# Weaving score steps with the transposes and values of other blocks, and leaving one softmax map undivided, in a two-layer attention and MLP trunk

## The chip, the cores and the metric

The kernel runs on one core of one Trainium2 chip. A core has a matrix engine (PE; its weight loads are listed apart as PEld), a vector engine (DVE), an activation engine (ACT), a general engine (POOL) and a queue for transfers (SP). Each takes its instructions in the order of its own queue; semaphores hold an instruction back until what it needs is there. Matrix products land in eight banks of a small memory (PSUM), each 128 x 512 numbers of 32 bits, and have to be read out by DVE or ACT before a bank is used again. The metric is the time of one execution in microseconds, the median of several.

## The reference

The input x has 512 tokens of 1024 numbers in float32. Each of two layers normalizes x, projects it, runs two kinds of attention heads on the parts, projects their joined outputs and adds them to x, and then adds a squared-ReLU MLP of width 4096. One more normalization follows at the end.

```python
h = rmsnorm(x, attn_norm[l])
sb_q, sb_k, sb_v, df_q, df_k, df_v = split(h @ w_in[l])       # 512 wide each
# stick-breaking heads (8 of 64): z = q k / 8, strictly causal
w = exp(log_sigmoid(z) + (sum over later keys of log_sigmoid(-z)))
sb_out = w @ v
# differential heads (4 of 2 x 64, values of 128), q and k rotated, causal by chunks of 64
p = softmax(s)                                                # two maps, p[0] and p[1]
attn = p[0] - lam * p[1]
df_out = rmsnorm(attn @ v, subln_norm[l]) * (1 - lambda_init)
x = x + concat(sb_out, df_out) @ w_o[l]
x = x + square(relu(rmsnorm(x, mlp_norm[l]) @ w_ff1[l])) @ w_ff2[l]
```

`rmsnorm(y)` is y / sqrt(mean(y * y) + 1e-6) times a gain.

## The kernel before

All of x stays on the chip, transposed: 8 tiles of 128 features by 512 tokens. To keep float32 accuracy on PE, an operand is split into a rounded high part (ACT, `split`, L207; weights L119) and the rest (DVE, L208; weights L120), and a product is three matmuls (`three`, L257 to L262): high by high, high by low, low by high. A projection block (`block`) takes one weight tile of 128 x 1024 through 8 such triples into a bank with the tag "mm". Weight tiles are loaded by SP three ahead and split two ahead.

A layer starts with the attention stage. A generator `dense` gives the projection blocks in the order of `ORDER`: for the four differential blocks b = 0 to 3 queries with keys (d) and values (w), then for the four stick-breaking blocks queries, keys (s) and values (u), and after them half of the output projection (`wo(1)`). When a projection is done, it is taken out of its bank. For d this is a rotation: DVE makes two products (L463, L464), POOL a difference and a sum (L472, then L471), ACT and DVE split the results, SP moves query and low key parts into stacked tiles (L437), and ACT copies the high key parts (L458). Values are transposed on PE (vT, L405), and split by ACT and DVE (L412, L413).

A second generator, `attn`, runs over 24 units: 8 differential ones (block b, half of the queries) and 16 stick-breaking ones (block, head, half). A unit goes through three parts. `s1` makes the scores for two query rows of 128 (S, L499 and L500; bank tag "s", two banks) and turns them into weights. For a differential unit (`s1_df`) DVE masks the scores (L539, L543) and takes the negated row maximum (L540, L544); ACT takes Exp and sums the row (L552); DVE takes the reciprocals of both sums (L558) and multiplies the second with minus lambda (L559); POOL multiplies map 0 with its reciprocal (L560); DVE adds the scaled map 1 (L561). For a stick-breaking unit ACT takes two sigmoids (L514, L515), DVE a running product (L517), POOL the final product (L520). `s2` transposes the weights on PE (T, L580; bank tag "t", two banks) and splits them; a unit of the first half has three transposes, one of the second half seven in two steps of four and three. `s3` multiplies them with the values (O, L608 to L611; tag "o"). In iteration i, `attn` runs `s1` of unit i, `s2` of unit i - 2 and `s3` of unit i - 3. After a differential block's two halves are through, its output is normalized over two iterations: `start_norm` calls `rms_a` (squares transposed on PE, rs_d; sums and scaling on DVE, L232 and L233; the power -1/2 on POOL, L238; its split on DVE, chi and clo, L239 and L240; two diagonals on POOL, L243 and L245), and `finish` spreads the result with two matmuls (rb_d, L253 and L254), a copy on ACT, a product on POOL (L660) and a split.

The loop at L739 weaves the two generators: after each dense triple `attn` gets a credit, and steps of `attn` are taken while it is positive. A `yield 0` means that what it needs isn't there yet. The text's order is not yet that of the queues: the framework's scheduler orders each engine's instructions by its own estimates of their times.

After the attention stage come the other half of the output projection (`wo(0)`) and the MLP (f, at 128 x 512 per matmul throughout).

Of the kernel before, what the change touches and what calls it, by code (L numbers as in the profile page):

```python
# [9 lines left out]
F32 = mybir.dt.float32  # L10
# [3 lines left out]
ALU = mybir.AluOpType  # L14
# [127 lines left out]
def trunk(ctx, tc, xT, w, gains, lamv, cos, sin, out):  # L142
# [83 lines left out]

    def rms_a(src, inv_n, col, name, eng, dgt):
        pt = bank("t", "rs_" + name)
        if RST and eng is not nc.gpsimd or RST == 2:
            for j in range(4):  # L230
                nc.tensor.transpose(pt[:, j * P : (j + 1) * P], src[:, j * P : (j + 1) * P], ident)
            nc.vector.tensor_reduce(out=ms, in_=pt.rearrange("p (j f) -> p j f", j=4), axis=AX.X, op=ALU.add)  # L232
            nc.vector.tensor_scalar(out=ms, in0=ms, scalar1=inv_n, scalar2=EPS, op0=ALU.mult, op1=ALU.add)  # L233
        else:
# [116 lines left out]
    for l in range(L):  # L351
        with ExitStack() as actx:
# [66 lines left out]
            dgs = {}  # L419
            heads = {}  # L420

            later = []
# [101 lines left out]
            def s1_df(u):  # L524
                b, half = u["b"], u["half"]
                st = {w: stacks[("d", b, w)] for w in "qk"}
                u["w"] = []
                for i in (2 * half, 2 * half + 1):
                    wd = P * (i + 1)
                    nm = f"{l}d{b}{i}"  # L530
                    sm = a3.tile([P, 6], F32, tag="sm", name="sm" + nm, bufs=4)
                    pr = []
                    both = bank("s", f"S{nm}") if wd <= 256 else None
                    for m in range(2):
# [13 lines left out]
                        if both is None or m == 1:  # L548
                            for mm, (pp, ss) in enumerate(pr):
                                if both is None and mm < m:  # L550
                                    continue
                                nc.scalar.activation(  # L552
                                    pp[:, 0:wd], ss[:, 0:wd], AF.Exp, bias=sm[:, mm : mm + 1],
                                    accum_out=sm[:, 2 + mm : 3 + mm])
                        if m == 0 and both is None:
                            yield max(wd, 256) * 2 * MMC
                    pr = [pp for pp, _ in pr]
                    nc.vector.reciprocal(sm[:, 4:6], sm[:, 2:4])  # L558
                    nc.vector.tensor_mul(sm[:, 5:6], sm[:, 5:6], nlam[:, l : l + 1])  # L559
                    nc.gpsimd.tensor_mul(pr[0][:, 0:wd], pr[0][:, 0:wd], sm[:, 4:5].to_broadcast([P, wd]))  # L560
                    nc.vector.scalar_tensor_tensor(  # L561
                        out=pr[0][:, 0:wd], in0=pr[1][:, 0:wd], scalar=sm[:, 5:6], in1=pr[0][:, 0:wd],
                        op0=ALU.mult, op1=ALU.add)
# [87 lines left out]
            def start_norm():  # L651
                b, os_, sqo, rc = late[0]
                dgs[b] = rms_a(sqo, 1.0 / P, rc, f"d{l}{b}", nc.gpsimd, tr)
                return 0.43

            def finish():
# [5 lines left out]
                return 0.43  # L662

            def attn():
                n = len(units)
                stage = 0
                for i in range(n + LAG3):
                    stage = stage + 1 if late else 0
                    if i < n:
                        u = units[i]  # L670
                        while not ok((u["kind"], u["b"])):
                            yield 0
                        yield from (s1_sb if u["kind"] == "s" else s1_df)(u)
                    if stage == 1:
                        yield start_norm()
                    if 0 <= i - LAG2 < n:
                        yield from s2(units[i - LAG2])
                    if stage == 2:
                        yield finish()
                        stage = 0  # L680
                    if 0 <= i - LAG3 < n:
                        while not ok(("v" + units[i - LAG3]["kind"], units[i - LAG3]["b"])):
                            yield 0
                        yield from s3(units[i - LAG3])

# [195 lines left out]
```

## Time and profile before

| | |
|---|---|
| median of 3 runs | 1228.05 us (1227.83 to 1228.29) |
| the profiled execution's own time | 1228.06 us |
| its span, first to last instruction | 1226.3 us |
| PE busy | 1194.8 us (97%), 5658 matmuls |
| DVE busy | 680.1 us (55%), 1016 instructions |
| ACT busy | 551.6 us (45%), 932 |
| POOL busy | 202.3 us (16%), 260 |

The span by stage, with PE's busy time in each:

| stage | us | PE busy |
|---|---|---|
| opening and first projections | 0 to 37 | 34.2 |
| layer 0, differential scores | 37 to 128.5 | 84.7 |
| layer 0, stick-breaking scores beside projections | 128.5 to 205.6 | 74.5 |
| layer 0, output projection | 205.6 to 262 | 56.4 of 56.4 |
| layer 0, MLP | 262 to 612 | 350 of 350 |
| layer 1, first projections | 612 to 640 | 28 of 28 |
| layer 1, differential scores | 640 to 728.5 | 82.1 |
| layer 1, stick-breaking scores | 728.5 to 805.6 | 74.5 |
| layer 1, output projection and MLP | 805.6 to 1200 | all |
| end | 1200 to 1226.3 | 16.0 |

Names in the profile: S0d is a score bank of layer 0 for differential heads, T1s a bank of transposes of layer 1 for stick-breaking heads, p0w2v a projection block (layer 0, values of block 2). A line such as "L552 p0d<-S0d" is the source line, what is written and what is read. Matmuls are pipelined: one of 128 x 512 is listed with 389 ns, but in a full stream the next starts 227 ns later. The granted clock is 1.00 where PE runs at full speed.

### The profile page before, as it was taken

Reading aid. Unit: us, or ns where it says so; the run is one execution under the profiler, and the core shown is the slowest. Engines: PE = TensorE matmul, PEld = TensorE weight load, DVE = VectorE, ACT = ScalarE, POOL = GpSimd, SP = SyncE. Lnnn points to the kernel's source line nnn. Section 1 sums busy time; section 2 is a strip of 40 time slices with the busy share of each in tenths; the row PEclk is TensorE's granted clock in tenths of the full one; section 3 lists DMA queues with packets and bytes.
Section 4 is the critical chain, followed back from the end, with each engine's and each line's share of the span. In section 5 each row is a group of like instructions: output and inputs, shape, how many; then the busy total and the mean of one; then the engine's idle time right before and its main releaser. Section 6 shows DMA issues by size and latency. Waiting matters only on the chain.

```text
span 1226.3 us, 15312 instructions
## 1 busy us (share of the span) xinstructions
PE 1194.8 (97%) x5658; PEld 991.6 (81%) x5658; DVE 680.1 (55%) x1016; ACT 551.6 (45%) x932; POOL 202.3 (16%) x260
## 2 busy tenths in 40 slices
PE   9989999999999999999998999999999999999996
PEld 6777878888888888888887788888888888888886
DVE  7778877764532334433367887886544322544325
ACT  5666665553431234423347765665443221443114
POOL 1313543230000000001122344432100000000002
PEclk9999999999999999999999999999999999999998
DMA  7344443222233232232234344432223233232221
GB/s 250 78 137 133 119 136 104 68 87 104 87 102 101 88 103 95 94 104 90 100 97 132 110 128 118 123 103 70 94 96 103 89 101 103 86 103 91 90 95 69
DMA packets 46890, 128.16 MB, mean 105 GB/s; under 512 B 7264, under 2 KB 10336, under 8 KB 46816
## 3 DMA queue, kind: packets, MB, share of 16 engines
q1 hardware_dynamic: 46672, 127.17, 33.0%
q8 instruction: 45, 0.74, 0.2%
q14 instruction: 29, 0.24, 0.1%
q10 hardware_dynamic: 144, 0.02, 0.0%
HBM read 104.09 MB, written 2.10 MB: 87 GB/s over the span
## 4 chain that ended last, share of the span: by engine, by line
PE 85%; DVE 4%; ACT 3%; POOL 2%; issue 1%; SPq 1%; DMA 0%; DVEq 0%; POOLq 0%; ACTq 0%
PE f L260 19%; PE f L262 19%; PE f L261 19%; PE wo L261 2%; PE wo L260 2%; PE wo L262 2%; DVE wlo L120 1%; SPq L437 1%; PE T1s L580 1%; PE T0s L580 1%; PE O1s L609 0%; PE O0s L609 0%; PE O1s L608 0%; PE O0s L608 0%; PE S1d L499 0%
## 5 line engine op out<-in xcount | busy, mean ns | idle before, releaser
L119 ACT ACTIVATE whi<-raw 128x1024 fp32r<-128x1024 f32 (+2 forms) x198 | 203.2, 1028 | 480.0 <-PE f L261 427.2
L120 DVE TENSOR_TENSOR wlo<-raw,whi 128x1024 fp32r<-128x1024 f32 (+2 forms) x198 | 242.0, 1224 | 147.1 <-ACT whi L119 146.2
L260 PE MATMUL f<-h_hi,whi 128*128 128x512 f32 x512 | 199.4, 389 | 0.0
L262 PE MATMUL f<-h_hi,wlo 128*128 128x512 f32 x512 | 199.2, 389 | 0.0
L261 PE MATMUL f<-h_lo,whi 128*128 128x512 f32 x512 | 199.2, 389 | 0.0
L260 PE MATMUL f<-uh,whi 128*128 128x512 f32 x496 | 192.9, 389 | 0.0
L261 PE MATMUL f<-ul,whi 128*128 128x512 f32 x496 | 192.9, 389 | 0.0
L262 PE MATMUL f<-uh,wlo 128*128 128x512 f32 x496 | 192.9, 389 | 0.0
L783 DVE SCALAR_TENSOR_TENSOR ft<-f,rbc 128x512 f32<-128x512 f32 x64 | 44.3, 692 | 163.8 <-PE f L262 162.8
L262 PEld LDWEIGHTS f<-h_hi,wlo 128*128 128x128 f32 x512 | 96.1, 188 | 20.1
L261 PEld LDWEIGHTS f<-h_lo,whi 128*128 128x128 f32 x512 | 96.1, 188 | 20.0
L260 PEld LDWEIGHTS f<-h_hi,whi 128*128 128x128 f32 x512 | 96.1, 188 | 19.8
L261 PEld LDWEIGHTS f<-ul,whi 128*128 128x128 f32 x496 | 93.1, 188 | 19.4
L262 PEld LDWEIGHTS f<-uh,wlo 128*128 128x128 f32 x496 | 93.1, 188 | 19.4
L260 PEld LDWEIGHTS f<-uh,whi 128*128 128x128 f32 x496 | 93.1, 188 | 19.2
L221 POOL TENSOR_TENSOR ssq<-ssq,sq 128x512 f32<-128x512 f32 x21 | 34.8, 1656 | 374.3 <-ACT sq L220 365.2
L812 DVE TENSOR_TENSOR x<-x,f 128x512 f32<-128x512 f32 x32 | 22.0, 688 | 103.0 <-PE f L262 103.0
L342 POOL TENSOR_TENSOR ssq<-ssq,sqf 128x256 f32<-128x256 f32 x6 | 4.4, 737 | 338.4 <-ACT sqf L340 335.0
L208 DVE TENSOR_TENSOR ul<-fu,uh 128x512 fp32r<-128x512 f32 x64 | 44.1, 692 | 0.4 <-ACT uh L207 0.4
L207 ACT ACTIVATE uh<-fu 128x512 fp32r<-128x512 f32 x64 | 40.6, 635 | 2.0
L784 ACT ACTIVATE fu<-ft 128x512 f32<-128x512 f32 x64 | 39.7, 620 | 1.6 <-DVE ft L783 1.6
L520 POOL TENSOR_TENSOR sig1s<-sig1s,C1s 128x128 f32<-128x128 f32 (+3 forms) x32 | 30.0, 939 | 55.3 <-DVE C1s L517 40.9
(725 smaller groups left out, 2173.5 us busy)
## 6 DMA issues: line engine op xcount, KB each, us to landing
raw<-in_w SPq DMA_DIRECT2D x176, 512.0 KB, 3.5
raw<-in_w SPq DMA_DIRECT2D x16, 448.0 KB, 3.1
x<-in_xT SPq DMA_DIRECT2D x8, 256.0 KB, 4.4
out_xT<-y SPq DMA_DIRECT2D x8, 256.0 KB, 2.4
raw<-in_w SPq DMA_DIRECT2D x8, 128.0 KB, 4.3
cos_t<-in_cos SPq DMA_DIRECT2D x2, 256.0 KB, 3.8
sin_t<-in_sin SPq DMA_DIRECT2D x2, 256.0 KB, 3.6
kl0d0k<-l0d0k SPq DMA_DIRECT2D x8, 64.0 KB, 2.0
```

The source lines that it names most:

```text
L119: h = nc.scalar.activation(hi[:, a:b], raw[:, a:b], AF.Copy)
L120: self.last = h, nc.vector.tensor_tensor(out=lo[:, a:b], in0=raw[:, a:b], in1=hi[:, a:b].bitcast(F32), op=ALU.subtract)
L207: nc.scalar.activation(hi, src, AF.Copy)
L208: nc.vector.tensor_tensor(out=lo, in0=src, in1=hi.bitcast(F32), op=ALU.subtract)
L221: return s, eng.tensor_tensor(out=ssq, in0=ssq, in1=sq, op=ALU.add)
L260: nc.tensor.matmul(pt, ah, bh, start=first, stop=False)
L261: nc.tensor.matmul(pt, ah, bl, start=False, stop=False)
L262: nc.tensor.matmul(pt, al, bh, start=False, stop=last)
L520: nc.gpsimd.tensor_mul(sig[:, 0:wd], sig[:, 0:wd], C[:, 1 : wd + 1])
L580: nc.tensor.transpose(pt[:, off : off + P], u["w"][qi][:, kb * P : (kb + 1) * P], ident)
L783: nc.vector.scalar_tensor_tensor(out=t, in0=pt, scalar=0.0, in1=rbc, op0=ALU.max, op1=ALU.mult)
L784: nc.scalar.activation(uu, t, AF.Square)
```

## The change

Two things are changed, both in the attention stage.

In `attn`, the parts of an iteration ran one after the other: all of `s1` of unit i, then the start of a norm, then `s2` of unit i - 2, then the end of a norm, then `s3` of unit i - 3. Now everything behind `s1` is a generator of its own, `behind_scores`, and one step of it is taken after each step of `s1`. What is left of it follows after the last one. The number of steps and what they compute are as before.

In `s1_df`, the maps are no longer divided by the first sum. Where the weights were e0 / t0 - lam e1 / t1, with e the exponentials and t their row sums, they are now e0 - lam (t0 / t1) e1, which is t0 times as much. POOL's multiplication of map 0 falls away; DVE takes one reciprocal instead of two, and the small product has one more factor. The head's output is t0 times too large, and the normalization that follows takes that out, if its constant 1e-6 is multiplied by t0 squared. The first sums are kept in a tile `top` (one column for each query row of 128), `start_norm` makes `floor` = 1e-6 t0 t0 from them on DVE, and `rms_a` adds it in place of the constant.

```diff
+    def rms_a(src, inv_n, col, name, eng, dgt, floor=None):
...
+            if floor is None:
+                nc.vector.tensor_scalar(out=ms, in0=ms, scalar1=inv_n, scalar2=EPS, op0=ALU.mult, op1=ALU.add)
+            else:
+                nc.vector.scalar_tensor_tensor(
+                    out=ms, in0=ms, scalar=inv_n, in1=floor, op0=ALU.mult, op1=ALU.add)
...
+                if half == 0:
+                    tops[b] = a3.tile([P, 4], F32, tag="top", name=f"top{l}{b}", bufs=3)
+                top = tops[b]
...
+                    sums = (top[:, i : i + 1], sm[:, 2:3])
...
-                                    accum_out=sm[:, 2 + mm : 3 + mm])
+                                    accum_out=sums[mm])
...
-                    nc.vector.reciprocal(sm[:, 4:6], sm[:, 2:4])
-                    nc.vector.tensor_mul(sm[:, 5:6], sm[:, 5:6], nlam[:, l : l + 1])
-                    nc.gpsimd.tensor_mul(pr[0][:, 0:wd], pr[0][:, 0:wd], sm[:, 4:5].to_broadcast([P, wd]))
+                    nc.vector.reciprocal(sm[:, 3:4], sums[1])
                     nc.vector.scalar_tensor_tensor(
-                        out=pr[0][:, 0:wd], in0=pr[1][:, 0:wd], scalar=sm[:, 5:6], in1=pr[0][:, 0:wd],
+                        out=sm[:, 4:5], in0=sums[0], scalar=nlam[:, l : l + 1], in1=sm[:, 3:4],
+                        op0=ALU.mult, op1=ALU.mult)
+                    nc.vector.scalar_tensor_tensor(
+                        out=pr[0][:, 0:wd], in0=pr[1][:, 0:wd], scalar=sm[:, 4:5], in1=pr[0][:, 0:wd],
                         op0=ALU.mult, op1=ALU.add)
...
             def start_norm():
                 b, os_, sqo, rc = late[0]
-                dgs[b] = rms_a(sqo, 1.0 / P, rc, f"d{l}{b}", nc.gpsimd, tr)
+                floor = a3.tile([P, 4], F32, tag="floor", name=f"floor{l}{b}")
+                nc.vector.scalar_tensor_tensor(
+                    out=floor, in0=tops[b], scalar=EPS, in1=tops[b], op0=ALU.mult, op1=ALU.mult)
+                dgs[b] = rms_a(sqo, 1.0 / P, rc, f"d{l}{b}", nc.gpsimd, tr, floor)
                 return 0.43
...
+            def behind_scores(i, stage):
+                n = len(units)
+                if stage == 1:
+                    yield start_norm()
+                if 0 <= i - LAG2 < n:
+                    yield from s2(units[i - LAG2])
+                if stage == 2:
+                    yield finish()
+                if 0 <= i - LAG3 < n:
+                    while not ok(("v" + units[i - LAG3]["kind"], units[i - LAG3]["b"])):
+                        yield 0
+                    yield from s3(units[i - LAG3])
+
             def attn():
...
+                    rest = behind_scores(i, stage)
                     if i < n:
...
-                        yield from (s1_sb if u["kind"] == "s" else s1_df)(u)
-                    if stage == 1:
-                        yield start_norm()
-                    if 0 <= i - LAG2 < n:
-                        yield from s2(units[i - LAG2])
+                        front = (s1_sb if u["kind"] == "s" else s1_df)(u)
+                        for cost in front:
+                            yield cost
+                            nxt = 0
+                            while nxt == 0:
+                                nxt = next(rest, None)
+                                if nxt is not None:
+                                    yield nxt
+                    yield from rest
                     if stage == 2:
-                        yield finish()
                         stage = 0
-                    if 0 <= i - LAG3 < n:
-                        while not ok(("v" + units[i - LAG3]["kind"], units[i - LAG3]["b"])):
-                            yield 0
-                        yield from s3(units[i - LAG3])
```

More of the change, by code (lines that the diff above doesn't have):

```diff
@@ L225, in behind @@
             mybir.DependencyClass.NoSync, mybir.DependencyReason.DATA), reason="order")
-    def rms_a(src, inv_n, col, name, eng, dgt):
+    def rms_a(src, inv_n, col, name, eng, dgt, floor=None):
         pt = bank("t", "rs_" + name)
@@ L232, in rms_a @@
             nc.vector.tensor_reduce(out=ms, in_=pt.rearrange("p (j f) -> p j f", j=4), axis=AX.X, op=ALU.add)
-            nc.vector.tensor_scalar(out=ms, in0=ms, scalar1=inv_n, scalar2=EPS, op0=ALU.mult, op1=ALU.add)
+            if floor is None:
[3 more added lines that the diff above has]
+                    out=ms, in0=ms, scalar=inv_n, in1=floor, op0=ALU.mult, op1=ALU.add)
         else:
@@ L420, in trunk @@
             heads = {}
+            tops = {}
             later = []
@@ L530, in s1_df @@
                     nm = f"{l}d{b}{i}"
-                    sm = a3.tile([P, 6], F32, tag="sm", name="sm" + nm, bufs=4)
+                    sm = a3.tile([P, 5], F32, tag="sm", name="sm" + nm, bufs=4)
+                    sums = (top[:, i : i + 1], sm[:, 2:3])
                     pr = []
```

## The prediction

> **What bounds the kernel now.** I read PE's busy time by stage, then PE's waits by releaser, then the timeline at each large one, then the clock. The busy time by stretch (us; then PE, PEld, DVE, ACT, POOL busy, granted clock):
>
> ```profile
> 37.00:128.50 91.50, 84.70 (x413) 69.44 (x412) 71.62 (x155) 64.36 (x136) 28.35 (x28) 0.96 0.45 127
> 128.50:205.60 77.10, 74.51 (x415) 62.83 (x413) 61.55 (x85) 48.59 (x98) 34.09 (x56) 1.00 0.43 116
> ...
> 640.00:728.50 88.50, 82.12 (x413) 68.20 (x412) 69.25 (x150) 59.34 (x126) 28.57 (x28) 0.98 0.43 128
> 728.50:805.60 77.10, 74.50 (x414) 62.77 (x412) 60.52 (x84) 48.61 (x98) 33.83 (x56) 1.00 0.43 116
> ```
>
> PE is the bound; outside these attention stretches it stands idle only at the two ends. Here it idles 6.8 + 2.6 + 6.4 + 2.6 = 18.4 us. Who it waits for (total, times, longest):
>
> ```profile
> PE S1d L499 <- ACT p1d L552: 6.4, 4, 3.0
> PE S0d L499 <- ACT p0d L552: 6.3, 5, 2.2
> ...
> PE rb_d L253 <- DVE zl L208: 2.0, 2, 1.0
> PE T1s L580 <- DVE vs L413: 1.6, 1, 1.6
> PE T0s L580 <- DVE vs L413: 1.6, 1, 1.6
> ```
>
> So scores wait for the Exp that frees one of their two banks. Why Exp is late, at the worst place of layer 0 (start, duration):
>
> ```profile
> 92.34 0.61 POOL L560 TENSOR_TENSOR p0d<-p0d,sm0d 128x256 f32<-128x256 f32 x1 [0.54 <-DVE sm0d L558]
> ...
> 92.90 1.21 DVE L120 TENSOR_TENSOR wlo<-raw,whi 128x1024 fp32r<-128x1024 f32 x1
> 92.93 2.32 POOL L471 TENSOR_TENSOR u0d3q<-u0d3q,v0d3k 128x512 f32<-128x512 f32 x1
> ...
> 94.03 1.50 DVE L561 SCALAR_TENSOR_TENSOR p0d<-p0d,sm0d,p0d 128x256 f32<-128x256 f32 x1
> ...
> 95.29 0.63 ACT L207 ACTIVATE h0d3k<-u0d3q 128x512 fp32r<-128x512 f32 x1 [2.57 <-POOL u0d3q L471]
> ...
> 98.61 0.70 PE L499 MATMUL S0d<-st0d2k,st0d2q 128*128 128x512 f32 x1 [2.16 <-ACT p0d L552]
> ```
>
> Exp stands on ACT behind a rotation copy (L207) that waits for POOL, and POOL and DVE shut each other out: L471 takes 1.28 alone (60.40) and 2.32 beside L120, L561 1.50 instead of 0.48. Last the clock, in two neighbouring stretches of 3.41 us:
>
> ```profile
> 95.33:98.74 3.41, 1.25 (x6) 0.69 (x5) 2.25 (x8) 3.33 (x7) 0.00 (x0) 1.00 0.24 59
> 98.74:102.15 3.41, 3.41 (x12) 2.82 (x13) 3.27 (x9) 2.90 (x7) 1.15 (x2) 0.50 0.74 234
> ```
>
> After a stretch with PE busy for 1.25 us, the next runs at half clock and costs 1.7. This happens three times (from 71.43, 98.74, 651.70; the stretch before had PE busy 1.40, 1.25, 0.51). The gap of 61.39 to 63.06 left no mark.
>
> **The change part by part.** I set each engine's queue in the two built kernels side by side. Removed: 32 POOL multiplications (L560), 8 x (0.40 + 0.61 + 0.83 + 1.28) = 25 us of POOL. Added: 8 floor instructions on DVE, 0.16 each by L559 (1.0 where POOL shuts it out), 1.3 to 8 us of DVE in all; they stand where DVE waits for Exp anyway, so I cost them at nothing; with that cover gone they push what DVE does next, which the terms below hold. The 32 reciprocals and small products stay. PE, ACT and SP get the same work; transposes and value matmuls issue no DMA. SP only swaps a weight load with rotation moves of block 3, twice a layer: a weight block feeds 5.4 us of PE and lands in 3.5, so nothing (without that slack up to 1.6 each). PE's order changes nowhere before 60 us, nor before 660 in layer 1: the 3.0 wait at 651.79 (five key copies on ACT and a table load of 1.28) and its half clock stay. All sums are against the profiled run's 1228.06 (span 1226.3 and 1.8 around it); the median is 1228.05, so nothing is corrected.
>
> *Layer 0, block 1 (60 to 71).* POOL goes from v0d2q (ends 59.66) straight on to u0d2q, which began at 60.40 behind L560: L207, Exp and the score of 63.06 come 0.7 earlier. From there ACT has 7.87 us of work in a row up to the Exp at 70.12, with 0.27 idle, so the score of 70.98 still waits about 2.1. Ahead by 0.95 in all; -0.3 if DVE takes the ports POOL left, -1.7 if the half clock goes too.
>
> *Layer 0, block 2 (88 to 99).* Exp of the second 384-wide score now precedes h0d3k on ACT. But DVE has, ahead of that score's maximum (L540), the norm's L232, its floor step, fl and the copy chi, which waits for POOL's power (1.0). By the rows: L120 to 94.8, POOL's u0d3q to 96.1, L561 to 96.3, L232 to 97.0, power to 98.35, chi 98.6, L540 99.15, Exp, score 99.9. On the way PE waits 1.8 at three transposes, whose bank L232 frees. PE has done 1.0 us more work by then (three projection matmuls, three transposes), so 99.9 compares with 98.61 + 1.0: +0.3 (-1.5 if DVE gets ahead of POOL, +1.3 if it is shut out twice). The idle time is now in two parts (1.8 and 1.15), so no half clock, at 3 in 4: -1.3 (-1.7 to 0).
>
> *The norm's broadcast (rb_d).* Block 1, layer 0: the copy of the value transposes now stands on ACT behind a table load (1.28) and two sigmoids, and rb_d waits for their bank: +0.9 (0 to 1.0). Block 3, both layers (164.93 and 764.9, each 1.15 late): zl now follows fl directly on DVE, and one more step lies ahead of rb_d; but POOL's second diagonal stands behind a 512-wide product (1.2), so 0.5 stays: -1.2 in all (-2.3 to 0).
>
> *T after the value transposes (185.33 and its like in layer 1, each 1.79 late).* Four of the transposes come two steps earlier and the other three wait for their fl instead of vs. On DVE mt 0.68, L120 1.22, vdl 0.67, scan 0.96, fl 0.68 in a row from 179.87 end at 184.1, where PE arrives at 183.15: with the restart 1.15 stays, -1.3 in all (-3.4 to +0.5).
>
> *Layer 1, block 1 (665 to 674).* Between the second 384-wide score and the 512-wide one stand nine projection and six value matmuls, where three projections and three transposes stood; 1.6 us more PE work by then, so 671.99 compares with 673.6. But ACT now has three key copies (1.92) ahead of that Exp, and they stand behind h1d2k, which waits for POOL's u1d2q. The score starts at 673.6 if POOL goes ahead of L120, at 675.1 if L120 does; with the next score: +0.8 (-1.0 to +1.7), and a half clock at 1 in 4: +0.4 (0 to 1.7).
>
> *Layer 1, block 2 (697.59, 2.26 late):* here both Exp precede the copies and both maxima chi; 0.6 stays, -1.65 (-2.26 to +0.5). *Block 3 (719.12, 0.69 late):* seven matmuls and a set of transposes more between the scores, -0.4 (-0.7 to +0.5).
>
> *Other woven spots.* T, rs_d and scores now stand nearer to what they wait for at some places; by the same rows most arrive within 0.2 us of it: +1.0 for both layers (0 to 3, about twice one T wait).
>
> Sum: -0.95 + 0.3 - 1.3 + 0.9 - 1.2 - 1.3 + 0.8 + 0.4 - 1.65 - 0.4 + 1.0 = -3.4, so **1224.7**. The ends add up to 1213.5 and 1238.
>
> [...]
>
> **The rivals.** *All the listed waits go*, and two half clocks: -14.6 at the ends, some -11, 1217. For it: three of the score waits hang on POOL's queue. Against: ACT is full between 61 and 70, and DVE's new order. *It cancels*, 1227.5: the weave moves waits from Exp to DVE's order, and taking L560 away frees an engine that is busy 28 of 91 us. For it: block 2 of layer 0, block 1 of layer 1. *Slower:* DVE's queue, in order. One chi, held by POOL's power, stands ahead of a maximum, so the next score, bank and transposes are late; at eight norms 1.0 each (8.0) and two new half clocks (3.4), less the 3.4 above: +8, 1236. It decides where chi holds DVE by 0.4 more at each norm than worked out above. Against: in layer 1, block 2, chi comes behind the maxima.
>
> *Transposes counted as idle by the clock.* Then a woven stretch with 1.7 idle and four transposes (0.45) falls too: two more half clocks, 1228.1. The stretch from 61.19 had 1.66 idle and a transpose and kept its clock; nothing here shows more. [...]
>
> **How the numbers follow.** Forecast (1219.5 to 1225.6) 0.39, all waits go 0.11, cancels 0.24, transposes 0.05, slower 0.21. A measurement here tells about 0.2% (2.5 us) from no change. Faster 0.39 + 0.11 = 0.50; same 0.24 + 0.05 = 0.29; slower 0.21. The range leaves out the far half of the two outer cases: 1216 to 1233; the forecast's own range is the one in brackets.
>
> **What would show it.** No L560, POOL some 25 us lower. The wait at 651.79 unchanged. The waits of S0d and S1d on ACT fall from 12.7 to about 11, those of rb_d and T on DVE from 5.2 to about 4 with one rb_d of 0.9 near 131 in layer 0; a new T0d wait of 1.8 near 96, on ms; two or three stretches at 0.50, none at 98.74. I am wrong if half clocks grow in number, if chi holds DVE longer than 1.1 in front of a maximum, or if ACT between 61 and 70 shrinks.

## The result, and the profile after

The changed kernel takes 1221.43 us (median of 6 runs, 1220.16 to 1223.12), the kernel before 1228.05. The ratio is 0.9952, with a 95% interval of 0.9942 to 0.9962: faster by about 6.6 us, where 1224.7 was forecast. The profiled execution took 1221.59 us, with a span of 1219.8.

The four attention stretches of the changed kernel, cut at the same projection blocks as those shown of before (us; then PE, PEld, DVE, ACT, POOL busy, granted clock):

```profile
37.00:123.15 86.15, 81.60 (x412) 66.25 (x411) 68.10 (x156) 63.55 (x134) 17.75 (x13) 1.00 0.47 134
123.15:198.60 75.45, 74.76 (x416) 63.58 (x415) 60.54 (x88) 49.69 (x101) 32.35 (x54) 1.00 0.44 120
633.85:723.30 89.45, 83.13 (x416) 68.14 (x415) 67.55 (x152) 58.48 (x124) 17.37 (x13) 0.98 0.42 127
723.30:798.50 75.20, 74.48 (x415) 62.96 (x412) 60.14 (x88) 49.65 (x101) 32.44 (x55) 1.00 0.45 121
```

Layer 0 lost 5.35 + 1.65 us, and its clock is 1.00 where it was 0.96. Layer 1 lost only 1.9 in its second stretch and got 0.95 longer in its first. So nearly all of the gain lies in layer 0. PE's waits by releaser (total, times, longest):

```profile
PE S1d L504 <- ACT p1d L561: 4.3, 2, 3.0
PE S0d L504 <- ACT p0d L561: 3.3, 4, 2.1
...
PE rs_m L231 <- POOL ssq L221: 1.3, 2, 0.7
PE rb_d L257 <- DVE vdl L417: 1.0, 1, 1.0
...
PE T0d L590 <- DVE S0d L548: 0.7, 1, 0.7
...
PE T0s L590 <- DVE fl0s L208: 0.7, 1, 0.7
```

The scores' waits on Exp fell from 12.7 to 7.6 and T's waits of 1.6 became 0.7. New are a T0d wait, one rb_d wait, in layer 1, and the wait of rs_m, the first sums of the MLP's norm, once a layer. POOL is busy 168.3 us, 34.0 less, where 25 was forecast; 3.6 of the rest are in the additions of squares (L221, 34.8 before, 31.2 now).

The clock: of the three stretches at half clock, one is left. In the same columns, two neighbouring stretches around the wait near 67, and the two around the wait of 3.0 near 642:

```profile
65.03:68.44 3.41, 2.42 (x17) 1.81 (x15) 3.09 (x8) 3.33 (x7) 0.00 (x0) 1.00 0.51 141
68.44:71.85 3.41, 2.29 (x16) 2.21 (x17) 2.31 (x11) 3.40 (x11) 0.00 (x0) 1.00 0.43 109
...
641.88:645.29 3.41, 0.74 (x4) 0.28 (x2) 0.91 (x2) 3.37 (x7) 0.00 (x0) 1.00 0.39 99
645.29:648.70 3.41, 3.10 (x8) 2.77 (x9) 2.08 (x10) 3.36 (x10) 0.00 (x0) 0.50 0.44 111
```

The wait near 67 is as long as the one of before was (2.36 in the stream of matmuls against 2.18), yet no half clock follows. It lies across the edge of two stretches, and each keeps PE busy for over 2.2 of its 3.41 us.

**Two sums.** Take the gap between two matmuls as the distance of their starts less the usual pitch (0.227 us for 512 columns), and keep the stretches at half clock apart. Then PE lost about 2.9 us less to gaps than before, nearly all of it in layer 0, and 3.6 us less to half clock (5.1 before, 1.5 now). Together that is the 6.5 by which the two profiled executions differ.

### The profile page after: what moved, and what is told of

It is laid out like the page before. It is cut to its first block, busy times and chain, and to the rows that moved or that the text cites. A ratio compares the mean times of both kernels' runs of the same rounds, so it can differ in the third digit from the quotient of the medians.

```text
span 1219.8 us, 15247 instructions
## 1 busy us (share of the span) xinstructions
PE 1193.0 (98%) x5658; PEld 989.2 (81%) x5658; DVE 684.8 (56%) x1024; ACT 550.2 (45%) x932; POOL 168.3 (14%) x228
## 5 line engine op out<-in xcount | busy, mean ns | idle before, releaser
L120 DVE TENSOR_TENSOR wlo<-raw,whi 128x1024 fp32r<-128x1024 f32 (+2 forms) x198 | 242.7, 1227 | 149.2 <-ACT whi L119 147.7
L221 POOL TENSOR_TENSOR ssq<-ssq,sq 128x512 f32<-128x512 f32 x21 | 31.2, 1485 | 379.6 <-ACT sq L220 370.5
L208 DVE TENSOR_TENSOR ul<-fu,uh 128x512 fp32r<-128x512 f32 x64 | 44.1, 692 | 0.4 <-ACT uh L207 0.4
L207 ACT ACTIVATE uh<-fu 128x512 fp32r<-128x512 f32 x64 | 40.5, 632 | 2.0
L212 DVE SCALAR_TENSOR_TENSOR h_lo<-x,g_all,h_hi 128x512 fp32r<-128x512 f32 x32 | 32.1, 1010 | 7.7 <-ACT h_hi L211 7.7
```

What stands on the lines that cost most here:

```text
L120: self.last = h, nc.vector.tensor_tensor(out=lo[:, a:b], in0=raw[:, a:b], in1=hi[:, a:b].bitcast(F32), op=ALU.subtract)
L207: nc.scalar.activation(hi, src, AF.Copy)
L208: nc.vector.tensor_tensor(out=lo, in0=src, in1=hi.bitcast(F32), op=ALU.subtract)
L212: return a, nc.vector.scalar_tensor_tensor(out=h_lo[:, c, :], in0=x[:, c, :], scalar=g, in1=h_hi[:, c, :].bitcast(F32), op0=ALU.mult, op1= ...
L221: return s, eng.tensor_tensor(out=ssq, in0=ssq, in1=sq, op=ALU.add)
```

## The experiments

By its granted clock of 0.50, I count a stretch of 3.41 us at half clock as the work of 1.71. That is an estimate: in the one from 98.74 of before, projection matmuls start 0.43 us apart, where the full stream has 0.227. I use it to take the clock out of single profiled executions: the last column but one is the profiled time less 1.71 for each such stretch. Two executions of the same changed kernel come out 0.9 apart in it, so less than 1 us says nothing there. The three kernels with key copies on POOL have the squares on DVE too.

| kernel | median us | ratio to before (95%) | profiled us | half-clock stretches | less clock | wait or gap, new or left |
|---|---|---|---|---|---|---|
| before | 1228.05 | 1 | 1228.06 | 3 | 1222.9 | S1d 3.0 |
| after | 1221.43 | 0.9952 (0.9942 to 0.9962) | 1221.59 | 1 | 1219.9 | S1d 3.0 |
| weave alone | 1224.27 | 0.9969 (0.9957 to 0.9980) | 1225.53 | 2 | 1222.1 | T0d 1.4, rs_d 1.2 |
| softmax alone | 1226.17 | 0.9990 (0.9980 to 1.0001) | 1226.22 | 3 | 1221.1 | scores 11.9 in all |
| after again | 1221.13 | 0.9947 (0.9935 to 0.9959) | 1220.69 | 1 | 1219.0 | as after |
| weave at differential scores | 1223.47 | 0.9965 (0.9953 to 0.9978) | 1223.47 | 1 | 1221.8 | T 4.7 in all |
| squares on DVE | 1220.76 | 0.9946 (0.9932 to 0.9960) | 1218.76 | 1 | 1217.1 | no rs_m |
| Exp table early | 1219.88 | 0.9935 (0.9922 to 0.9947) | 1220.13 | 1 | 1218.4 | S1d 3.0 still |
| chi late | 1220.58 | 0.9942 (0.9930 to 0.9955) | 1220.76 | 2 | 1217.3 | S0d 1.9 near 94 |
| these three | 1220.10 | 0.9940 (0.9927 to 0.9952) | 1219.32 | 1 | 1217.6 | as chi late |
| key copies, block 1 | 1218.23 | 0.9930 (0.9917 to 0.9942) | 1217.81 | 0 | 1217.8 | S0d 2.1 near 67 |
| key copies, all blocks | 1218.22 | 0.9927 (0.9915 to 0.9940) | 1218.22 | 1 | 1216.5 | S0d 2.0 near 53 |
| squares, Exp table | 1221.84 | 0.9948 (0.9934 to 0.9962) | 1224.05 | 3 | 1218.9 | S1d 3.0 |
| key copies, two places | 1217.83 | 0.9916 (0.9902 to 0.9931) | 1217.87 | 1 | 1216.2 | S1d 1.9 |

### Which half of the change does it

The weave alone is the kernel before with only the change in `attn`; the softmax change alone is the changed kernel with `attn` as before.

> The weave alone; both softmax maps are divided by their own sums as before (reciprocals, the small product and the POOL multiplication L560 are back), the norm adds its constant again. My theory (the weave takes the waits of T behind the value transposes, splits the idle time at block 2 of layer 0 so that its half clock goes, and the POOL work taken away gives about 0.7 at block 1 and less elsewhere): 1223.5 to 1225.5, that is two thirds of the gain or more; T0s and T1s waits near 0.9 instead of 1.79, the first 2.2 wait of S0d on p0d in layer 0 (68.7) still there, no half clock after block 2. Rival (the gain is POOL's 25 us): 1226.5 to 1228, with scores still late by 2 behind Exp at block 2 in one piece and a half clock behind it.

> The softmax change alone, scores in the order of before. My theory: 1225.5 to 1227.5: L560 gone, POOL 25 us lower, the wait at 61 shorter by 0.7 and the waits of scores on Exp a little shorter in each block, T0s and T1s still 1.79 each, three half clocks still (two, if the wait at block 2 of layer 0 falls under 2). Rival (POOL's work is the gain): 1222 to 1224, with score waits on ACT at 8 or less instead of 12.7. If the two parts simply add, the gains of this kernel and of the weave alone sum to 6.6.

Measured by the medians: -3.6 for the weave, -1.7 for the softmax change (its interval just reaches no change), -6.7 for both in the same comparison. The first expectation's time and its two T waits are right (gaps of 0.96 at both), but its reading is not: the weave is just over half of the gain and not two thirds. Without the clock it is worth 0.8 and the softmax change 1.8, by one execution each. What the weave brings by itself in these profiles is mostly a half clock: the idle time at block 2 of layer 0 is one gap of 2.36 with the softmax change alone, and a half clock follows, but with the weave it is two gaps, of 1.18 and 0.91, and none does.

The two halves add up to 5.3 of the 6.7. The 1.4 left over is no more than the three intervals allow, so the times don't show that the halves help each other. One place in the traces does. The timeline of the weave alone, where the first transposes of block 0's second half are now due:

```profile
59.13 0.83 POOL L560 TENSOR_TENSOR p0d<-p0d,sm0d 128x384 f32<-128x384 f32 x1
59.92 1.27 POOL L471 TENSOR_TENSOR u0d2q<-u0d2q,v0d2k 128x512 f32<-128x512 f32 x1
...
60.00 1.60 DVE L561 SCALAR_TENSOR_TENSOR p0d<-p0d,sm0d,p0d 128x384 f32<-128x384 f32 x1 [0.20 <-POOL p0d L560]
...
61.66 0.33 PE L580 MATMUL T0d<-edge,p0d 128*128 128x128 f32 x1 [1.39 <-DMA raw<-in_w]
```

The wait is put down to a transfer, but the operand p0d was finished by DVE at 61.60. DVE waited for POOL's multiplication and then ran 1.60 beside POOL's rotation step. The gap there is 1.55; with both changes it is 0.43, since L560 is gone. The weave brings the transposes nearer to weights that the softmax change makes earlier.

### The same kernel again, and the weave in half of the places

> The changed kernel once more, nothing else. Theory (the windows over which the clock gate counts, 3.41 us long, lie differently in each execution): the times spread again over 1220 to 1223, and where the profile shows the gap of 2.36 us near 67 inside one window, a half clock of 3.41 us follows and the time is 1.7 longer than in the profile at hand; the idle gaps themselves stay the same within 0.1. Rival (the windows do not matter, the gap of 67 is below a threshold of its own): one half clock only, behind 642, whatever the window edges.

> The changed kernel with the weave at softmax scores alone; behind the sigmoid scores of the second half (from 128 and 728 on) the transposes and values come after both scores, as before. My theory: 1222.5 to 1224, since the T0s and T1s waits come back at 1.79 and 1.15 each layer in place of 0.95 (+0.8 to +1 a layer), and the first half keeps its gain of about 4. Rival (the first half gives nothing but a lucky clock, and the gain is in the second half): 1225 or more.

The second kernel differs from the changed one in one line:

```diff
                         for cost in front:
                             yield cost
-                            nxt = 0
+                            nxt = 0 if u["kind"] == "d" else None
                             while nxt == 0:
```

The repeat's times lie within those of the first runs, and the gaps over 0.3 in its attention stages are the same within 0.1. Outside them one differs: the wait of rs_m in layer 0 is absent, which the next section takes up. The 3.41 us of the theory are the length of the half clocks in the traces (71.44 to 74.85 before, 645.29 to 648.71 after); that PE's work counts by such stretches was still to be tested. The gap near 67 lay across an edge of two stretches again, so the repeat decided nothing on the clock. The other kernel did. It has the same two gaps, 2.36 near 67 and 3.14 near 644, at other places in the stretches:

```profile
66.40:69.82 3.42, 1.29 (x9) 0.90 (x8) 2.46 (x8) 3.38 (x11) 0.00 (x0) 1.00 0.44 110
69.82:73.23 3.41, 3.41 (x15) 3.26 (x14) 3.22 (x11) 3.41 (x8) 0.00 (x0) 0.50 0.39 98
643.25:646.66 3.41, 1.53 (x7) 0.94 (x5) 1.70 (x5) 3.37 (x5) 0.00 (x0) 1.00 0.39 99
646.66:650.07 3.41, 2.31 (x11) 1.86 (x12) 2.25 (x10) 3.40 (x12) 0.00 (x0) 1.00 0.41 103
```

Here the gap of 2.36 is inside one stretch, PE is busy for 1.29 of it, and the next runs at half clock. The gap of 3.14 is split between two stretches, and none follows, where in the ten other profiles that have a gap of 3.1 or more at this place one does. So here it isn't the length of a gap that counts but how much of it falls into one stretch. The first theory holds, its rival (a threshold for the gap) falls.

On the weave: 1223.47 against 1221.13 on the same chip, so the weave among the sigmoid scores is worth 2.3, within the expectation. But T did not go back to one wait of 1.79 and one of 1.15 in each layer; there are three gaps in each, of 0.7 to 1.1. Without the clock this kernel is no faster than the softmax change alone (1221.8 against 1221.1). By place, the gaps of the differential stages are smaller by some 0.7 and those of rb_d in block 3 are gone (2.3), but the gaps of T are larger (5.7 against 3.6). So the weave among the differential scores, on which most of my terms stood, gave little idle time back within its own stage. Its rival in this form, "a lucky clock and the second half", is nearer than I was.

### The new wait of rs_m

> The changed kernel with the running sum of squares of the output projection (L221 under wo(0)) added on DVE and not on POOL. My theory of the new waits of rs_m (0.83 in each layer, behind the last POOL addition, which ran in the same stretch as DVE's h_lo and both were slow): the waits of rs_m go and nothing replaces them, -1.6, about 1219.5. Rival (the last column of squares is simply late, by ACT's Square or by DVE's queue): the wait stays, now on DVE, 1221 or more.

```diff
-                            add_sq(db, db == 0, tt)
+                            add_sq(db, db == 0, tt, nc.vector)
```

In the changed kernel's timeline, behind the output projection of layer 0:

```profile
259.21 1.37 POOL L221 TENSOR_TENSOR ssq<-ssq,sq 128x512 f32<-128x512 f32 x1 [0.85 <-ACT sq L220]
259.37 1.76 DVE L212 SCALAR_TENSOR_TENSOR h_lo<-x,g_all,h_hi 128x512 fp32r<-128x512 f32 x1
...
260.64 0.66 PE L231 MATMUL rs_m<-edge,ssq 128*128 128x128 f32 x4 [0.67 <-POOL ssq L221]
```

With the additions on DVE at 0.68 each, h_lo takes 0.74 instead of 1.76, and both waits of rs_m are gone, with nothing in their place: gaps fell by about 2.4 against the first profile of the changed kernel and by about 1.6 against the repeat, which has only the wait of layer 1. That POOL and DVE slow each other is as expected. But the wait doesn't belong to every execution. The first of POOL's additions starts beside an h_lo on DVE; here in the changed kernel, in its repeat, and in the kernel before:

```profile
240.99 1.87 DVE L212 SCALAR_TENSOR_TENSOR h_lo<-x,g_all,h_hi 128x512 fp32r<-128x512 f32 x1
241.02 1.28 POOL L221 TENSOR_TENSOR ssq<-ssq,sq 128x512 f32<-128x512 f32 x1 [16.65 <-ACT sq L220]
```

```profile
240.85 0.75 DVE L212 SCALAR_TENSOR_TENSOR h_lo<-x,g_all,h_hi 128x512 fp32r<-128x512 f32 x1
240.88 1.86 POOL L221 TENSOR_TENSOR ssq<-ssq,sq 128x512 f32<-128x512 f32 x1 [16.65 <-ACT sq L220]
```

```profile
248.00 0.75 DVE L212 SCALAR_TENSOR_TENSOR h_lo<-x,g_all,h_hi 128x512 fp32r<-128x512 f32 x1
248.08 1.82 POOL L221 TENSOR_TENSOR ssq<-ssq,sq 128x512 f32<-128x512 f32 x1 [17.19 <-ACT sq L220]
```

Where h_lo is the slow one, the next x, its square and every later addition are late, and the last addition ends at 260.58. Where POOL is the slow one it ends at 259.06, before PE needs it. DVE starts first in all three, by 0.08 in the kernel before and by 0.03 in the changed one. In the eight profiles with these additions on POOL, six such meetings are 0.03 apart, all in kernels with both changes, and three of them went against DVE; ten are 0.04 to 0.08 apart, and none did. So the change brings the two instructions closer, and what follows is a matter of chance, as with the clock. That fits a smaller gain than 1.6. The median of five, 1220.76, moved by less than the 1.6 expected, and four of the five executions lie at 1220.3 to 1221.3; how many half clocks those had, no profile shows.

### The wait of 3.0 in layer 1

> The changed kernel with one Exp of a 128x1 column on ACT in the MLP of layer 0, so that the Exp table is loaded there and not in front of the first Exp of layer 1. My theory: the wait of S1d on p1d near 642 falls by the 1.28 of the table load, from 3.0 to about 1.7, too short for a half clock at any place of the windows (busy at least 1.5 of 3.41), so -1.3 and, in three executions of four, another -1.7: 1218 to 1220. Rival (the score waits for the key copies or for the rotation, and the table load lies beside that): the wait stays at 2.5 or more, 1221.

```diff
                             rms_b(rbc, f"m{l}", dg)
+                            if l == 0:
+                                nc.scalar.activation(prime, rbc[:, 0:1], AF.Exp)
```

ACT's part of the timeline, up to the Exp that frees the bank:

```profile
639.37 3.18 ACT L463 ACTIVATE st1d1k<-h1d1k 32x512 fp32r<-32x512 f32 x5
642.56 0.37 ACT L561 ACTIVATE p1d<-S1d,sm1d 128x128 f32<-128x128 f32 x1
```

The table load is gone from here, and the score starts at 643.42, where it started at 645.60. Yet the wait is 3.0 as before, so the rival's number holds, though not for its reason. The scheduler that orders the queues had put ten projection matmuls of p1d2q ahead of this score; now it put four. PE arrives 2.2 earlier (0.8 of it from a wait of rs_m that is absent in layer 0) and waits as long. What the table load cost was given back by the order. Both rs_m waits are absent in this profile, with the same order of ACT, POOL and DVE there as in the repeat's layer 0, and their 1.7 is enough for the gain over the changed kernel. The same with the squares on DVE:

> The changed kernel with the sum of squares on DVE and the Exp table loaded in the MLP. The first look at the table alone left the wait near 642 at 3.0, because six projection matmuls had moved behind it. Theory: the same order again, so no gain beyond the sum of squares: 1219 to 1220.5, wait near 642 of 3.0. Rival: the wait falls to 1.8 and the time to 1218 or less.

The wait is 3.0 again, as the theory has it, and the rival falls. The time, 1221.84 (1219.64 to 1224.05), is above the theory's range; its profiled execution, the slowest of the five, has three half-clock stretches, two of them in a row.

### Chi out of DVE's way

> The changed kernel with the norm of the softmax heads in two parts: transposes, sum, floor and power first, the copies chi and clo and the diagonals only after the transposes of the unit that is due (behind the second score), so that no maximum on DVE stands behind a chi that waits for POOL's power. My theory: the waits at 92 (T0d, 0.9) and 94.6 (S0d, 0.9) shrink together by 0.5 to 1.2, rb_d has the diagonals later and its waits grow by 0 to 0.6 in some blocks: 1220 to 1222. Rival one (chi is what costs, at every norm): 1219 or less. Rival two (the two waits come from POOL and DVE holding each other up at u0d3q, L120 and L571): both stay as they are, and rb_d's later diagonals make it 1222 to 1224.

```diff
         nc.gpsimd.tensor_tensor(out=col, in0=ms, in1=mhalf, op=ALU.pow)
+        if dgt is None:
+            return None
+        return rms_c(col, name, eng, dgt)
+
+    def rms_c(col, name, eng, dgt):
         nc.vector.tensor_copy(chi, col)
...
                 if 0 <= i - LAG2 < n:
                     yield from s2(units[i - LAG2])
+                if stage == 1:
+                    mid_norm()
```

First the changed kernel's own timeline at block 2 of layer 0, then that of this kernel:

```profile
89.75 1.22 DVE L120 TENSOR_TENSOR wlo<-raw,whi 128x1024 fp32r<-128x1024 f32 x1
89.78 2.33 POOL L476 TENSOR_TENSOR u0d3q<-u0d3q,v0d3k 128x512 f32<-128x512 f32 x1 [1.49 <-DVE v0d3k L469]
...
90.89 1.51 DVE L571 SCALAR_TENSOR_TENSOR p0d<-p0d,sm0d,p0d 128x256 f32<-128x256 f32 x1
...
94.33 0.17 DVE L243 CAST chi<-rc 128x4 fp32r<-128x4 f32 x1 [0.53 <-POOL rc L242]
94.41 0.55 DVE L549 TENSOR_REDUCE sm0d<-S0d 128x1 f32<-128x384 f32 x1
```

```profile
93.66 0.55 DVE L554 TENSOR_REDUCE sm0d<-S0d 128x1 f32<-128x384 f32 x1
94.28 0.63 ACT L207 ACTIVATE h0d3k<-v0d3q 128x512 fp32r<-128x512 f32 x1
94.94 0.63 ACT L468 ACTIVATE st0d3k<-h0d3k 32x512 fp32r<-32x512 f32 x1
...
95.96 0.58 ACT L566 ACTIVATE p0d<-S0d,sm0d 128x384 f32<-128x384 f32 x1
```

In the changed kernel chi does stand in front of the maximum, held 0.53 by POOL's power. Taken away, the maximum runs 0.75 earlier by the clock of the trace, about 0.5 against PE's work, and the score is later for it: a gap of 2.08 instead of 0.90. The scheduler now has the split of the rotation and a key copy on ACT ahead of the Exp. None of the three expectations names this. The T0d gap stayed at 0.89, as in rival two. The time, 1220.58, did not get worse, because other gaps are absent: vT and rb_d near 700 (0.64 and 1.16), against one rb_d of 1.34 at 724.70, and rs_m in both layers, where DVE won. With the squares on DVE and the early table as well:

> The last three edits together on the changed kernel. If they add up as in my theory: 1216.5 to 1218.5, with no half clock but the one behind the 2.36 gap near 67 in half of the executions. Rival (waits move on): 1219 or more.

1220.10: the gains don't add up. Its gaps are those of the chi kernel, 2.09 near 94 and 3.2 near 640.

### Whose work fills ACT

> The changed kernel with the sum of squares on DVE (as before in this study) and, for block 1 alone, four of the eight key copies (L463, 0.63 each) on POOL instead of ACT. It tests that the wait of 2.1 near 67 is a full ACT. My theory: ACT loses 2.5 between 61 and 70, the wait falls to 1.2 or less, no half clock follows it in any execution, and the wait of 1.5 near 665 falls by half too: 1217.5 to 1219.5. Rival (POOL's copies are slow and hold the rotation, or the planner puts other work in ACT's free time): the wait stays at 2 or moves to the score of block 1 that needs the keys, 1220 or more.

> The same with those four copies of every block on POOL (16 in each layer, 10 us of ACT a layer). Theory: the wait of 3.0 near 642 falls by the 1.3 to 1.9 of two or three copies as well, and its half clock goes in most executions: 1214.5 to 1218. Rival: POOL, with 16 more instructions a layer, is late for the rotations, the diagonals and the products with C: new waits on POOL of 1 or more, 1219.5 or more.

```diff
-                                defer(KC_GAP * (4 * j + 2 * m + i + 1), copy_k(k[d_, m, :], hi[rk, :]))
+                                defer(KC_GAP * (4 * j + 2 * m + i + 1), copy_k(k[d_, m, :], hi[rk, :], b == 1 and j == 1))
```

with `copy_k` made to use `nc.gpsimd.tensor_copy` where its last argument is true; `j == 1` alone in the second.

Block 1 was the wrong block for layer 0: the copies on ACT ahead of the wait near 67 are those of block 2 (st0d2k), so that wait stayed at 2.36, and the run says nothing on it. The gap of 1.5 near 665 stayed too, and near 53 one of 0.45 grew to 1.24. So the time, 1218.23, is within the theory's range without its reasons. In layer 1 block 1 is the right one: the gap near 642 went from 3.14 to 2.10, and no half clock followed in this profile. With all blocks on POOL it is the same 2.10, a fall of 1.0 where 1.3 to 1.9 was expected, and the time of 1218.22 is 0.2 above the theory's range. The gap near 67 went from 2.36 to 0.92, as the theory has it, but near 53, where it had been 0.45, there is now one of 2.15:

```profile
51.66 3.83 POOL L464 CAST st0d1k<-h0d1k 32x512 fp32r<-32x512 f32 x4 [5.61 <-ACT h0d1k L207]
51.76 1.59 DVE L120 TENSOR_TENSOR wlo<-raw,whi 128x1024 fp32r<-128x1024 f32 x1
```

POOL's four copies slow L120 from 1.22 to 1.59 and the L208 behind it from 0.69 to 1.09, and so the maxima and Exp are late. That is 0.8 of the 1.7 by which this gap grew. With block 1 alone on POOL the two are slowed the same, and the gap grew by 0.8 only. The rest goes with the order: here ACT has a fourth key copy ahead of the values' copy vdh, and DVE's row starts 0.8 later against PE. That led to the last kernel, with the copies on POOL at the two places alone where ACT is what PE waits for:

> The changed kernel with the sum of squares on DVE and four key copies on POOL at two places alone: block 2 of layer 0, whose copies stood on ACT in front of the wait near 67, and block 1 of layer 1, whose copies stood in front of the wait near 642. Theory (those two waits are a full ACT; with the copies of block 1 of layer 0 back on ACT nothing new is late near 53): waits of at most 1.0 near 67 and 2.1 near 642, none over 0.5 near 53, and 1215.5 to 1217.5. Rival (POOL's copies keep DVE from its maxima at the new place as they did near 53): a wait of 1 or more near 67, 1218 or more.

```diff
+                                defer(KC_GAP * (4 * j + 2 * m + i + 1), copy_k(k[d_, m, :], hi[rk, :], j == 1 and b == 2 - l))
```

Its waits of scores on Exp are 3.3 in layer 1 (2 times, 1.9 the longest) and 1.2 in layer 0 (3 times, 0.7). It takes 1217.83 us, a ratio of 0.9916 (0.9902 to 0.9931) to before: the lowest here, though the intervals of the two kernels above overlap it, and some 3.5 to 4 us below the changed one. The gap near 67 (0.92, now for a projection bank's weight), the one near 640 (2.09) and the absence of one near 53 (0.44) are as expected; the time is 0.3 above the range. Two of its executions took 1215.83, the others 1217.8 to 1218.1, about one half clock more.

## Why the prediction was right, and where its sum was off

The direction held, and so did the wide range of 1216 to 1233 and the forecast's own of 1219.5 to 1225.6. The upper end of the second is the sum with both clock terms left out, and no run shows why they should be: in the profile of before, the waits of 2.0, 2.2 and 3.0 that end at 70.98, 98.61 and 651.79 each had a half clock with them, and in that of after one is left. The sum said -3.4 and it was -6.6. By its own steps, in gaps between matmuls:

| step | forecast | measured |
|---|---|---|
| layer 0, block 1 | -0.95 | -1.4 |
| layer 0, block 2 | +0.3 | -0.9 |
| rb_d in layer 0, block 1 | +0.9 | 0 |
| rb_d in block 3, both layers | -1.2 | -2.3 |
| T after the value transposes, both layers | -1.3 | -1.7 |
| layer 1, block 1 | +0.8 | +0.5 |
| layer 1, block 2 | -1.65 | -0.5 |
| layer 1, block 3 | -0.4 | 0 |
| other spots | +1.0 | +3.4 |
| sum without the clock | -2.5 | -2.9 |
| half clocks | -0.9 | -3.6 |

That the gaps' sum is only 0.4 off is luck in good part: single steps are off by up to 2.4, in both directions, and cancel. Of the signs that I named, L560 is gone, the wait of 651.79 is unchanged (now at 645.60), and none of the three signs of being wrong came. But the scores' waits fell to 7.6 and not to about 11, those of rb_d and T to 2.4 and not to about 4, the rb_d wait came in layer 1 and not near 131, T0d waited half as long as said, and one stretch at 0.50 is left, not two or three.

**The term that was mis-sized is the clock.** Two of three half clocks went, where my terms were -1.3 at block 2 and +0.4 in layer 1. Block 2 went as worked out: the idle time is split, and the stretch there has PE busy for 1.98. What I had at nearly nothing (-1.7 as one end of block 1's range) is the half clock behind the wait near 67. That it went in the profile at hand isn't owed to the change: the wait is there in full, and in the kernel with half of the weave a half clock follows it. I took the three half clocks of the profile of before for a property of the kernel; they are that only as far as a gap's length makes it likely to fall into one stretch. The runs of before beside the first four experiments spread from 1225.4 to 1231.2, about three half clocks.

How likely a place is to make a half clock can be estimated from the traces. Slide a stretch of 3.41 us over PE's busy time and take the share of the placements in which PE is busy for less than 1.52, the bound worked out in the last section. Before, four places have such placements: near 68 (0.48 of them), 95 (0.52), 648 (0.76) and 695 (0.49), 2.3 half clocks in all. After, those near 67 (0.51) and 642 (0.76) are left, 1.3 in all. With the weave alone it is 1.2, with the softmax change alone 2.5. So what the change takes away, through the weave, is the chance at block 2 of both layers, about one half clock or 1.7 us, and by this estimate it is luck that the profile of after lacks a second one. Yet the medians of two groups of runs (-6.6 and -6.7) are nearer to two, so how much of the clock's 3.6 lasts is left open.

**Layer 0, block 1.** The 0.7 at L207 came (a gap of 1.83 became 0.42), and ACT is as full behind it as I read it (3.33 of 3.41 us busy in the stretch from 65.03), so the wait near 67 stayed. The run with block 2's copies on POOL, in which the gap there went from 2.36 to 0.92, shows that it is ACT's copies. The ports of the -0.3 are not shown: the traces have only the times, as 2.33 for POOL's L476 beside L120 (89.78) and 1.29 at 59.23.

**Layer 0, block 2.** I had POOL's rotation step get ahead and L120 take until 1.9 after its start. L120 was first: 1.22, with POOL at 2.33, the end of the range that I had noted and not taken. So L232 came 0.85 earlier against PE, T0d waited 0.9 and not 1.8, and the next score 0.9 and not 1.15. Chi was held 0.53 here, not over the 1.1 that would have decided for the slower case.

**rb_d.** In block 1 of layer 0 the wait didn't come. The same kind of wait, for the bank that the value transposes' copy frees (vdl), came in block 2 of layer 1 at 703.43 (a gap of 1.16), with 0.64 more at the value transposes. It ate most of what I had put down for that block: the scores' wait of 2.26 itself went to nothing, so my 0.6 that stays was too much and the wait behind it was not seen. In block 3 both rb_d waits went whole.

**T.** 1.79 became 0.94 and 0.96, where I had 1.15 stay, for the reason given: fl, at the end of DVE's row.

**Other spots.** The small gaps of the attention stages grew by 1.7 for both layers, inside my 0 to 3. The other 1.7 is the wait of rs_m, twice 0.83 in the profile at hand. I had PE idle only in the attention stages and at the two ends, and costed nothing outside them. DVE and POOL meet in the output projection before and after, but in the kernel before POOL is the slow one (1.82, h_lo 0.75), and nothing waits. With the change they start closer together, and in the profile at hand DVE was the slow one in both layers, in the repeat in one. So the step that failed is the one that put nothing outside the attention stages: not a wait in the change, but one behind it, and not in every execution. What in the change brings the two closer is left open.

**The rivals.** That all the listed waits go and two half clocks with them: two half clocks did go, and of the listed waits some 6. It cancels: no, though layer 1 by itself nearly does (0.95 over its two stretches, of which the wait of rs_m takes 0.8 back). Slower by chi on DVE: chi's hold is real but short, and taking it away gained nothing. Transposes as idle: it falls, but not by the stretch from 61.19 that I set against it, for that one holds no transpose (the first is at 64.81). In the kernel with chi late, rows of one execution:

```profile
67.47:70.88 3.41, 1.57 (x11) 1.54 (x12) 2.30 (x10) 3.39 (x11) 0.00 (x0) 1.00 0.44 111
...
94.78:98.19 3.41, 1.51 (x8) 1.29 (x9) 2.82 (x8) 3.31 (x7) 0.00 (x0) 1.00 0.71 239
98.19:101.60 3.41, 3.41 (x13) 2.72 (x12) 2.90 (x6) 3.35 (x7) 0.00 (x0) 0.50 0.42 107
```

The stretch from 67.47 kept its clock with 1.57 busy, and in it are four value transposes, busy for 0.60 by themselves and beside their neighbours for 0.4 of the 1.57. Without them it would have 1.0 to 1.4, by how the overlap is counted, less than stretches that lost theirs. With the softmax change alone, the stretch from 779.98 kept its clock with 1.83, of which 1.40 without transposes. The one from 94.78 had 1.51 and no transposes, and lost its clock. So by these rows the float32 transposes count as busy.

The edges of the clock's stretches in the profiles of before and after lie on a grid of 3.41 us. The first is at full clock for 64.85, 23.89, 549.55 and 563.20 us at a time, which is 19, 7, 161 and 165 times 3.413, and the second for 638.29 and 563.20, which is 187 and 165 times. Where the grid lies differs by execution: the clock first goes to 1.00 at 6.58 us of the span in the profile of before, at 7.00 in that of after, and at 4.17 to 6.80 in the others.

## What to carry to other kernels

Read a half clock in one profile as a chance and not as a cost: see how much of the gap falls between two edges, and price the gap by how often that happens (the gap of 2.36 near 67 had no half clock behind it in two executions of the changed kernel, and one in the kernel with half of the weave). When a change shortens one stage, look also at the stages behind it that it doesn't touch, because the same work can meet other neighbours there, and profile the same kernel twice before a wait is put down to the change. Where a scheduler orders the queues, look at the order after each edit: an instruction taken out of one engine's way may let others in ahead of the one that was to gain.

## What the runs showed of the hardware

**What makes a half clock.** Over the 14 profiled executions, leaving out the two ends, each of the 20 stretches at full clock of 3.41 us in which PE was busy for 0.42 to 1.51 us was followed by one at half clock, and none of those at full clock with 1.53 or more was. So in these runs the bound lies between 1.51 (the stretch from 94.78 of the kernel with chi late) and 1.53 (the one from 643.25 of that with the weave at differential scores); 1.52 of 3.41, 45%, is my estimate from the two, with transposes counted. A gap of 2.08 was enough where it lay in one stretch (chi late, near 94), and one of 3.14 had none behind it where it lay in two (weave at differential scores, near 644). One stretch that was itself at half clock, with PE busy for 2.6 of it, was followed by another at half clock; the 20 others, with 3.1 or more, were followed by full clock. What between these it takes to come back is left open.

**DVE and POOL.** Which of two that start together is slowed varies, even in the same kernel: beside an addition on POOL that starts 0.03 later, h_lo took 1.87 in one execution of the changed kernel and 0.75 in the repeat. Beside L476, L120 took its usual 1.22 and POOL 2.33; beside POOL's key copies L120 took 1.59 and POOL 0.92 for a copy on average, against 0.61 in block 3 of layer 1. Which one starts first doesn't settle it: in the pair at 89.75 and 89.78 DVE is 0.03 ahead and POOL is held up, in the pair at 240.99 and 241.02 DVE is 0.03 ahead too, by the starts that the profile lists, and is itself held up.

**A table load for Exp** took 1.28 us (at 649.63 in the profile of before). With it moved away, the wait near 642 stayed at 3.0.
